# The sample's recurrence beside the prompt's projections, and half of w_out fetched during the prompt's recurrence

## The chip, the core and the metric

The kernel is one program on one core of a Trainium2 chip. The metric is the device time of one execution in microseconds; the time before is the median of three executions. The engines are TensorE (PE, the matrix products), VectorE (DVE), ScalarE (ACT), GpSimd (POOL) and SyncE (SP); SP and POOL issue nearly all of the transfers between the chip's main memory and the engines' memory.

## What is computed

A trunk of two layers runs over two requests with the same weights: a prompt of 1024 rows and a sample of 256 rows, 1024 columns each, all in float32. The sample doesn't depend on the prompt. In one layer:

```python
h = rms_norm(x, norm1_w[l])
proj = h @ w_in[l]                      # 1024 x (5*640 + 3*384)
q_h, zf, zb, i_h, g_h, q_a, k_a, v_a = split(proj)
hg_out = hgrn2_mixer(q_h, zf, zb, i_h, g_h, ...)    # gated recurrence, both directions, 5 heads of 128
at_out = dilated_attention_mixer(q_a, k_a, v_a)     # windowed attention, 3 groups of 2 heads
x = x + concatenate([hg_out, at_out]) @ w_out[l]
x = x + expert_choice_moe(rms_norm(x, norm2_w[l]), ...)   # 16 experts, each takes its best rows
```

The recurrence needs of `w_in` the columns q_h, zf, zb (640 each), of the same rows the values i_h and the gates g_h, and gives 640 of the 1024 columns that go into `w_out`; the attention gives the other 384.

## The kernel before

A product in float32 accuracy is made of three faster ones: each operand X is split into a rounded part H (made by ACT) and a rest L (made by DVE), and PE adds H·H, H·L and L·H. So a weight block costs a load (`raw`, `wr` or `or`), an ACT pass (`wH`, `oH`) and a DVE pass (`wL`, `oL`), and each product is three matmuls per 128 rows of depth.

`mixers` issues one layer's first half in this order. The program is written as streams (Python generators); `lanes` and `run_all` take from each stream in turn by an estimate of when its next PE work can start, and that fixes the order of each engine's instructions. Every engine and every queue of transfers then works through its own instructions strictly in that order. A stream that has to wait for another yields in `until` on a key of a dictionary.

1. **Projections** (`project`, L517, with `value_tile` L545 and `qkv_tile` L558). Four column blocks of 320 (values and gates of the recurrence, `mm<-wH,hTh` with 128x320 outputs) and three of 384 (attention) for both requests, a tile of 128 rows at a time: 8 tiles of the prompt, 2 of the sample. Results go to `vgp`, `vgs`, `qkvp`, `qkvs` in main memory. `order` lists the blocks; the sample runs some blocks ahead.
2. **The prompt's recurrence** (`hgrn` L578, `hgrn_task`, `hgrn_unit`), 5 heads times 2 units of 512 rows. A unit projects its own q and z (`mm<-hTh,wH`, 128x512, with the head's weights from `load_head` L593, whose raw tile `wr` has one buffer), then goes through levels: `lv<-qk`, five times `lv<-Q,km`, then `lv<-Q,K`, then a 128-row level, each of which waits for DVE products (`update`) and an ACT copy (`km`) of the one before; then states S, and outputs `tp<-v,A` and `tp<-S,Q`. They are squared, normalised (`hss`, `rs*`), multiplied by the gates `sg` (loaded at L648, one buffer) into `hob`, and stored by POOL (L1108) as `mbp`. Two units run at a time. Beside it run the 30 **attention** units (24 of the prompt, 6 of the sample), paced by `int(i * 0.2)` against the recurrence's progress `first`; their results are stored by SP (L930) as `obp`, `obs`.
3. **The sample's recurrence**, the same with 5 units of 256 rows (`lv<-hTh,wH`, 128x256). It waits for `projected` (the prompt's last projection is done) and `attended` (all attention is issued), so it starts about where the prompt's last unit has its levels, and goes on into the next stage. `out_weights` (L939) makes `oH` and `oL` from 16 loads of w_out through two `or` buffers at the same time.
4. **The output projection** (`out_proj` L979, `row_tile`): for each of 8 prompt tiles, then 2 sample tiles, load the mixed rows (`mix<-mbp` L1000, `obr<-obp` L1002, `x` L1005, by SP), weigh the attention (`aM`, `aw`), transpose, split (`mTh`, `mTl`), multiply by w_out (`mm<-oH,mTh`), add, norm, router logits. After the prompt's 8 tiles comes its expert choice (`topk_merged`, first instruction MAX8), then the experts.

Lines that most DVE and ACT instructions carry are those of a helper (L111); PE's are L182 (matmul) and L196 (transpose).

## Time and profile before

| | us |
|---|---|
| time, median of three executions (3395.47 to 3405.37) | 3402.97 |
| span of the profiled execution, first to last instruction | 3399.2 |
| PE busy in it | 3255.7 (96%) |
| DVE busy | 2113.0 (62%) |
| ACT busy | 1763.4 (52%) |
| mean granted TensorE clock, as a share of full speed | 0.978 |

The profile holds the span alone and no time around it; the span lies within the range of the timed executions, 3.8 us under their median. Matmuls overlap, so the duration shown for one is longer than its distance to the next: the cost of a row of equal matmuls is read from their starts. The stages in the span, by the first and last instructions of each kind: projections 26 to 290, the prompt's recurrence 290 to 634, the stretch up to the first product with w_out 634 to 704, the rest of the output projection up to the expert choice 704 to 869; in the second layer the last two are 2315 to 2388 and 2388 to 2556.

### The profile page before, as it was taken

The page shows a single profiled execution, that of the slowest core. Times are in us where ns is not written, and L with a number is a line of the kernel's source. Part 1 is how long each engine was busy: PE and PEld are TensorE (multiplying, and loading weights), DVE is VectorE, ACT ScalarE, POOL GpSimd, SP SyncE. Part 2 cuts the span into 40 slices and gives each one's busy share as a digit, 9 for nine tenths or more (in the row PEclk, how much of TensorE's full clock was granted, in tenths as well). Part 3 has the DMA queues.
Part 4 walks back from the last instruction along what each step waited for, and adds up shares of the span by engine and source line. Part 5 has one row for each costly group of instructions (what it writes and reads, how often), then busy time and mean ns, then how long its engine had stood idle before and what let it go on. Part 6 is the DMA issues. An engine that isn't in the chain of part 4 may idle for free.

```text
span 3399.2 us, 59013 instructions
## 1 busy us (share of the span) xinstructions
PE 3255.7 (96%) x23714; PEld 2485.4 (73%) x23714; DVE 2113.0 (62%) x4201; ACT 1763.4 (52%) x2533; POOL 270.4 (8%) x225
## 2 busy tenths in 40 slices
PE   8999999889899999999999999998997999999996
PEld 8998777777666667666699977777775666667664
DVE  5322677885866666666543137788757766666666
ACT  4214774553356666566532156745424665666665
POOL 0000000000111111111100000000001111111102
PEclk9999999899899999999999999998998999999998
DMA  5213222344498889888642132214434988888887
GB/s 180 91 56 89 64 75 60 113 149 127 171 326 281 286 284 323 297 281 284 218 149 89 55 101 67 65 48 134 146 122 170 325 319 287 284 286 312 303 284 251
DMA packets 423969, 641.88 MB, mean 189 GB/s; under 512 B 31376, under 2 KB 191760, under 8 KB 423696
## 3 DMA queue, kind: packets, MB, share of 16 engines
q1 hardware_dynamic: 398544, 557.88, 47.3%
q0 software_dynamic: 24432, 77.61, 8.3%
q8 instruction: 187, 3.06, 0.4%
q10 hardware_dynamic: 720, 2.62, 0.2%
q14 instruction: 86, 0.70, 0.1%
HBM read 551.13 MB, written 86.89 MB: 188 GB/s over the span
## 4 chain that ended last, share of the span: by engine, by line
PE 42%; DVE 3%; DMA 3%; ACT 1%; issue 1%; SPq 0%; POOLq 0%; ACTq 0%; DVEq 0%
PE mm L182 22%; PE lv L182 9%; PE sc L182 6%; PE tp L196 3%; PE tp L182 2%; DMA wr<-in_w_in_dram 1%; DVE wL L111 1%; DMA obr<-obp 0%; ACT wH L111 0%; DVE raw L111 0%; DVE ind L111 0%; DMA xbp<-ye,idxp 0%; DVE val L111 0%; DVE lv L111 0%; DMA xeS<-xns,gidx 0%
## 5 line engine op out<-in xcount | busy, mean ns | idle before, releaser
L111 DVE TENSOR_TENSOR wL<-raw,wH 128x2048 fp32r<-128x2048 f32 (+2 forms) x412 | 917.2, 2244 | 401.6 <-ACT wH L111 401.4
L111 ACT ACTIVATE wH<-raw 128x2048 fp32r<-128x2048 f32 (+2 forms) x412 | 774.4, 1882 | 189.1 <-PE mm L182 92.6
L182 PE MATMUL mm<-wH,hTh 128*128 128x320 f32 (+1 forms) x1120 | 361.1, 323 | 1.4 <-ACT hTh L111 1.3
L182 PE MATMUL mm<-wL,hTh 128*128 128x320 f32 (+1 forms) x1120 | 359.9, 321 | 0.3 <-DVE wL L111 0.3
L182 PE MATMUL mm<-wH,hTl 128*128 128x320 f32 (+1 forms) x1120 | 359.6, 321 | 0.0
L182 PE MATMUL sc<-raw,xs 128*32 128x512 f32 x2048 | 230.9, 597 | 0.0
L182 PEld LDWEIGHTS mm<-wH,hTh 128*128 128x128 f32 x1120 | 210.6, 188 | 2.3 <-ACT hTh L111 2.3
L182 PEld LDWEIGHTS mm<-wL,hTh 128*128 128x128 f32 x1120 | 210.6, 188 | 0.5 <-DVE wL L111 0.5
L182 PEld LDWEIGHTS mm<-wH,hTl 128*128 128x128 f32 x1120 | 210.5, 188 | 0.3 <-DVE hTl L111 0.2
L182 PE MATMUL mm<-wL,xh 128*128 128x512 f32 x512 | 205.3, 401 | 1.6 <-DVE wL L111 1.6
L182 PE MATMUL mm<-wH,xh 128*128 128x512 f32 x512 | 205.4, 401 | 0.0
L182 PE MATMUL mm<-hTh,wH 128*128 128x512 f32 x480 | 203.0, 423 | 0.0
L182 PE MATMUL lv<-wL,xh 128*128 128x512 f32 x512 | 200.1, 391 | 2.1 <-DVE wL L111 2.1
L182 PE MATMUL mm<-wH,xl 128*128 128x512 f32 x512 | 201.1, 393 | 0.0
L182 PE MATMUL lv<-wH,xh 128*128 128x512 f32 x512 | 199.5, 390 | 0.0
L182 PE MATMUL lv<-wH,xl 128*128 128x512 f32 x512 | 199.5, 390 | 0.0
L182 PE MATMUL mm<-hTh,wL 128*128 128x512 f32 x480 | 199.0, 415 | 0.3 <-DVE wL L111 0.3
L182 PE MATMUL mm<-hTl,wH 128*128 128x512 f32 x480 | 196.4, 409 | 0.0
L1264 POOL DMA_INDIRECT xbs<-yS,sidx x64 | 101.8, 1591 | 1120.5 <-ACT yS L111 976.5
L182 PEld LDWEIGHTS sc<-raw,xs 128*32 128x32 f32 x2048 | 64.4, 110 | 147.4 <-issue 144.7
L182 PE MATMUL sc<-raw,hs 128*32 128x512 f32 x1024 | 150.6, 598 | 0.0
L111 DVE TENSOR_TENSOR K<-K,TT 128x256 f32<-128x256 f32 (+1 forms) x360 | 126.1, 376 | 30.1 <-PE lv L182 19.1
(291 smaller groups left out, 6486.0 us busy)
## 6 DMA issues: line engine op xcount, KB each, us to landing
raw<-in_w_up_dram SPq DMA_DIRECT2D x128, 1024.0 KB, 15.6
raw<-in_w_down_dram SPq DMA_DIRECT2D x128, 1024.0 KB, 9.4
raw<-in_w_gate_dram SPq DMA_DIRECT2D x126, 1024.0 KB, 13.8
wr<-in_w_in_dram SPq DMA_DIRECT2D x60, 512.0 KB, 4.0
raw<-in_w_in_dram SPq DMA_DIRECT2D x16, 640.0 KB, 5.7
vgp<-vgo SPq DMA_DIRECT2D x64, 160.0 KB, 1.8
raw<-in_w_in_dram SPq DMA_DIRECT2D x12, 768.0 KB, 5.3
qkvp<-qo SPq DMA_DIRECT2D x48, 192.0 KB, 1.9
```

The source lines that it names most:

```text
L111: return fn(out, *args, **kw)
L182: self.last_mm = self.nc.tensor.matmul(out, lhsT, rhs, start=start, stop=stop)
L196: ins = self.nc.tensor.transpose(out, src, self.ident[:k, :k])
L1264: nc.gpsimd.indirect_dma_start(out=xs2, out_offset=at, in_=yS[64 * h:64 * h + 64], in_offset=None, compute_op=OP.add)
```

## The change

- `project` yields within its tiles (`mm3` becomes the stream `mm3y`), and the sample's recurrence runs beside it, right after the prompt's rows are normalised: a new state of two keys, `v` and `g`, tells it when the sample's values and gates are stored. The sample's fourth block is moved into the middle of the prompt's third.
- The sample's recurrence is gone from behind the prompt's. Its head weights use the projections' `raw` buffers (two, which were three); the prompt's still use one `wr`. The order of heads is now sample first, then prompt.
- Attention is paced by `min(10, int(i * 0.4))`, which leaves units 25 to 29 waiting for the prompt's last unit.
- `out_weights` has eight `or` buffers instead of two and issues the first eight loads at the start of the prompt's recurrence; all 16 passes of ACT and DVE still come after `projected`.
- The pools (regions of on-chip memory) are entered in another order.

The docstrings and comments that the change deletes are left out of this diff.

```diff
@@ mixers
-            hTs = self.new_hT(gs, left.enter_context(pool("hTs")))
-            proj = ExitStack()
+            proj, projs, blk = ExitStack(), ExitStack(), ExitStack()
             hTp = self.new_hT(gp, proj.enter_context(pool("hTp")))
-            with pool("rawA", "right") as rw, pool("wA", "right") as wa, \
-                    pool("stage", "right") as sp, pool("norm1", "right") as xp:
-                wp = (rw, 3, wa, 4)
+            hTs = self.new_hT(gs, projs.enter_context(pool("hTs")))
+            rw, wa, sp = (blk.enter_context(pool(n)) for n in ("rawA", "wA", "stage"))
+            state = dict(normed=0, all_normed=0, v=0, g=0, s=0, best=0, started=0, turned=0, multiplied=0, ended=0,
+                         projected=0, attended=0, scanned=0, loaded=0, p=0, merged=0)
+            wp = (rw, 2, wa, 4)
+            with pool("norm1", "right") as xp:
...
-                state = dict(normed=0)
-                self.run_all(self.project(l, hTs, hTp, sp, wp, first, state, 2),
-                             self.norm_in(l, gp, hTp, xp, w1, junk, state))
+                projecting = self.project(l, hTs, hTp, sp, wp, first, state, 2)
+                self.run_until(state, ("all_normed",), projecting, self.norm_in(l, gp, hTp, xp, w1, junk, state))
...
-            gp.next, gs.next = gs, None
+            self.head_raw = rw, "raw", 2
+            gs.next, gp.next = gp, None
+            gp.ps, gp.ps_name, gs.ps, gs.ps_name = self.mmp, "mm", self.lvp, "lv"
             for j in range(3):
-                self.load_head(l, gp, 0, j)
+                self.load_head(l, gs, 0, j)
+
+            def sample_hgrn():
+                with pool("hgrns", "right") as hg:
+                    yield from self.hgrn(l, gs, hTs, hg, ready=state)
+
+            self.run_all(sample_hgrn(), projecting)
+            blk.close()
+            projs.close()
...
+            orw = right.enter_context(pool("orw", "right"))
...
             def load_weights():
-                yield from self.until(state, "projected", 1)
-                yield from self.out_weights(l, *weights[0])
+                yield from self.out_weights(l, orw, weights, state)
                 state["loaded"] = 1
-            def sample_hgrn():
-                yield from self.until(state, "projected", 1)
-                yield from self.until(state, "attended", 1)
-                with pool("hgrns") as hg:
-                    yield from self.hgrn(l, gs, hTs, hg)
-                state["s_scanned"] = 1
...
@@ project
+        order.remove((3, gs))
+        order = [(b, g, range(g.T)) for b, g in order]
+        n = order.index((2, gp, range(gp.T)))
+        order[n:n + 1] = [(2, gp, range(0, 4)), (3, gs, range(gs.T)), (2, gp, range(4, 8))]
...
+            if g is gs and b in (1, 3):
+                state["v" if b == 1 else "g"] = 1
@@ value_tile, qkv_tile
-        self.mm3(ps, self.top(hT, P * i, P), self.wop(blk, 0, 320))
+        yield from self.mm3y(ps, self.top(hT, P * i, P), self.wop(blk, 0, 320))
@@ load_head
-        raw = wp.tile([P, 8, P], F32, name="wr")
+        rp, nm, bufs = self.head_raw
+        raw = rp.tile([P, 8, P], F32, name=nm, bufs=bufs)
@@ hgrn_task
         yield 150.0
+        yield from self.until(hd["ready"], "g", 1)
@@ hgrn_unit
         yield from self.until(state, "tails", (i - 2) // NU + 1)
+        yield from self.until(hd["ready"], "v", 1)
...
+        if NU == 1:
+            yield from self.until(state, "tails", i)
@@ attention
-            yield from self.until(scan, "first", int(i * 0.2))
+            yield from self.until(scan, "first", min(10, int(i * 0.4)))
@@ out_weights
-            raw = pool.tile([P, 512], F32, name="or", bufs=2)
+            raw = pool.tile([P, 512], F32, name="or", bufs=8)
...
-        load(0)
-        load(1)
-        yield 3000.0
+        for i in range(8):
+            load(i)
+        yield from self.until(state, "projected", 1)
+        H, L = weights[0]
         for i in range(16):
...
-            if i < 14:
-                load(i + 2)
+            if i < 8:
+                load(i + 8)
```

Where the order of instructions changes (first layer). **PE in the prompt's projections**, where values and gates are made; before, one tile after another:

```order
600 L182 MATMUL mm<-wH,hTh 128x320
601 L182 MATMUL mm<-wL,hTh 128x320
602 L182 MATMUL mm<-wH,hTl 128x320
603 L182 MATMUL mm<-wH,hTh 128x320
604 L182 MATMUL mm<-wL,hTh 128x320
```

PE at the same place now, where `lv`, `tp<-v,kt` and `tp<-ident,K` belong to the sample's recurrence:

```order
486 L182 MATMUL mm<-wL,hTh 128x320
487 L182 MATMUL mm<-wH,hTl 128x320
488 L182 MATMUL tp<-v,kt 128x128
489 L196 MATMUL tp<-ident,K 128x128
490 L182 MATMUL lv<-Q,km 32x32 x8
491 L182 MATMUL mm<-wH,hTh 128x320
492 L182 MATMUL mm<-wL,hTh 128x320
493 L182 MATMUL mm<-wH,hTl 128x320
```

The sample's level products stand 6 to 26 projection matmuls apart, and its last unit ends 732 matmuls ahead of the end of the projections.

**PE from the first level of the prompt's last unit on**; before, the sample's projections (128x256) stand between the levels:

```order
2855 L182 MATMUL lv<-hTl,wH 128x256
2856 L182 MATMUL lv<-hTh,wL 128x256
2857 L182 MATMUL lv<-qk 32x32 x16
2858 L182 MATMUL lv<-hTh,wH 128x256
2859 L182 MATMUL lv<-hTl,wH 128x256
2860 L182 MATMUL lv<-hTh,wL 128x256
```

Now what stands between the last levels is the last attention units (`qkvr`, `kT`, `sc`, `qT`):

```order
3252 L182 MATMUL lv<-Q,K 32x32 x9
3253 L196 MATMUL tp<-ident,qT 128x128
3254 L182 MATMUL lv<-Q,K 32x32 x7
3255 L196 MATMUL tp<-ident,qkvr 128x128 x2
3256 L182 MATMUL sc<-kT,qT 128x128 x2
3257 L182 MATMUL lv<-Q,km 128x128 x4
3258 L196 MATMUL tp<-ident,qkvr 128x128 x2
3259 L196 MATMUL tp<-ident,K 128x128 x2
3260 L182 MATMUL sc<-kT,qT 128x128 x2
3261 L196 MATMUL tp<-ident,K 128x128
```

And on PE the output projection's first transposes (`mix`) follow the unit's last outputs at once:

```order
3281 L182 MATMUL tp<-S,Q 128x128 x2
3282 L182 MATMUL tp<-v,A 128x128
3283 L182 MATMUL tp<-S,Q 128x128
3284 L196 MATMUL tp<-ident,mix 128x128 x4
3285 L182 MATMUL mm<-oH,mTh 128x512
```

Between the last unit's `lv<-qk` and these transposes there are 50 attention matmuls, and none of the sample's recurrence.

**SP's queue at the end of the prompt's recurrence**; before, w_out's and the sample's weight loads come ahead of the first mixed rows:

```order
184 L604 DMA wr<-in_w_in_dram 128x8x128 x2
185 L950 DMA or<-in_w_out_dram 128x512 x2
186 L604 DMA wr<-in_w_in_dram 128x8x128
187 L950 DMA or<-in_w_out_dram 128x512 x3
188 L648 DMA sg<-vgp 128x4x128
189 L950 DMA or<-in_w_out_dram 128x512
190 L761 DMA v<-vgs 128x2x128
191 L604 DMA wr<-in_w_in_dram 128x8x128
192 L1000 DMA mix<-mbp_85 128x512
```

SP at the same place now:

```order
181 L967 DMA or<-in_w_out_dram 128x512 x8
182 L863 DMA qkvr<-qkvs 16x3x128 x5
183 L947 DMA obs<-ao 128x132
184 L947 DMA obs<-ao 64x132 x4
185 L863 DMA qkvr<-qkvs 16x3x128 x3
186 L947 DMA obs<-ao 16x132 x16
187 L662 DMA sg<-vgp 128x4x128
188 L1018 DMA mix<-mbp_85 128x512
189 L1018 DMA mix<-mbp_86 128x128
190 L1020 DMA obr<-obp 128x3x132
```

The second half of w_out's loads stands ahead of the last attention unit's loads, and the attention's last 16 stores stand ahead of the last gates and the first mixed rows. The number of PE instructions is the same before and after (18266).

## Rows read from the trace of the kernel before

**Rows 1.** The page: the span.

```profile
span 3399.2 us, 59013 instructions
```

**Rows 2.** Busy time by stretch: start:end, length, engines busy (x instructions), PEclk, DMA share, GB/s.

```profile
100.00:150.00 50.00, 50.00 (x343) 50.00 (x342) 17.68 (x32) 8.99 (x16) 0.00 (x0) 1.00 0.28 94
295.90:302.70 6.80, 6.80 (x26) 5.63 (x26) 3.27 (x12) 5.40 (x16) 0.00 (x0) 0.50 0.57 161
...
634.00:704.30 70.30, 50.67 (x720) 45.02 (x720) 58.28 (x188) 34.20 (x72) 4.20 (x6) 0.84 0.52 155
2315.40:2387.80 72.40, 52.32 (x717) 46.13 (x717) 62.98 (x195) 36.00 (x74) 3.51 (x5) 0.79 0.48 140
704.30:869.20 164.90, 160.68 (x1253) 125.48 (x1254) 107.35 (x440) 67.80 (x166) 11.53 (x20) 0.99 0.40 127
2387.80:2556.40 168.60, 162.24 (x1253) 125.23 (x1254) 108.44 (x456) 66.96 (x164) 12.25 (x21) 0.98 0.41 128
```

**Rows 3.** The chain of waits, second layer, 2310 to 2400: start us, us, what.

```profile
2325.17 4.62 DMA wr<-in_w_in_dram
```

**Rows 4.** PE's timeline in the output projection: start us, us, instruction, x pieces.

```profile
720.36 0.39 PE L182 MATMUL tp<-v,A 128*128 128x128 f32 x2
...
721.35 0.33 PE L182 MATMUL lv<-Q,km 128*32 128x32 f32 x16
...
722.19 0.28 PE L182 MATMUL lv<-hTl,wH 128*128 128x256 f32 x1
...
724.43 0.28 PE L182 MATMUL lv<-hTh,wL 128*128 128x256 f32 x1
...
728.99 0.28 PE L182 MATMUL lv<-hTh,wH 128*128 128x256 f32 x1
729.20 0.33 PE L182 MATMUL lv<-Q,km 128*32 128x32 f32 x16
...
729.69 0.28 PE L182 MATMUL lv<-hTh,wL 128*128 128x256 f32 x1
```

**Rows 5.** The sample's matmuls ahead of 634 (580 on) and of 2315.4 (2260 on).

```profile
L182 PE MATMUL lv<-hTh,wH 128*128 128x256 f32 x13 | 3.7, 287 | 0.0
...
L182 PE MATMUL lv<-hTh,wH 128*128 128x256 f32 x15 | 4.1, 276 | 0.0
```

**Rows 6.** PE's timeline: router's last matmul of two tiles, two tiles apart.

```profile
837.83 0.38 PE L182 MATMUL sc<-ident,re 128*16 128x128 f32 x2
...
868.46 0.39 PE L182 MATMUL sc<-ident,re 128*16 128x128 f32 x2
```

**Rows 7.** DVE by form, 634 to 690: xcount | busy us, mean ns | idle before.

```profile
L111 DVE TENSOR_TENSOR oL<-or,oH 128x512 fp32r<-128x512 f32 x14 | 9.4, 684 | 0.0
...
L111 DVE TENSOR_TENSOR K<-K,TT 128x256 f32<-128x256 f32 x12 | 4.6, 418 | 0.1
L111 DVE TENSOR_TENSOR Q<-Q,TT 128x512 f32<-128x512 f32 x6 | 4.1, 681 | 0.0
...
L111 DVE SCALAR_TENSOR_TENSOR S<-S,T 128x128 f32<-128x128 f32 x9 | 2.7, 345 | 0.0
```

**Rows 8.** Timelines of ACT, DVE and POOL behind the prompt's last outputs [idle before <-releaser].

```profile
680.10 1.09 ACT L111 ACTIVATE hob<-tp 128x512 f32<-128x512 f32 x2 [0.36 <-PE tp L182]
...
690.35 1.13 DVE L111 SCALAR_TENSOR_TENSOR hob<-tp,rsy,sg 128x128 f32<-128x128 f32 x4 [0.33 <-DMA sg<-vgp]
...
692.01 0.75 POOL L1108 DMA_DIRECT2D mbp<-hob  x1 [3.51 <-ACT S L111]
...
2380.34 0.75 POOL L1108 DMA_DIRECT2D mbp<-hob  x1 [3.51 <-DVE K L111]
...
2389.64 0.16 DVE L111 TENSOR_TENSOR aM<-obr 128x2 f32<-128x2 f32 x1 [1.08 <-DMA obr<-obp]
```

**Rows 9.** DMA issues, 634 to 704: xcount, KB each, median us to landing.

```profile
obr<-obp SPq DMA_DIRECT2D x2, 198.0 KB, 8.2
sg<-vgp SPq DMA_DIRECT2D x1, 256.0 KB, 3.0
```

More of the change, by code (lines that the diff above doesn't have):

```diff
@@ L87 @@
 class Wait(float):
+    pass
 class Engine:
@@ L445, in after_projections @@
                 op = left.enter_context(pool("wout"))
-                weights.append((op,) + tuple(op.tile([P, 8, D], F32R, name=n) for n in ("oH", "oL")))
+                weights.append(tuple(op.tile([P, 8, D], F32R, name=n) for n in ("oH", "oL")))
                 state["projected"] = 1
@@ L484, in mixers @@
                 pools = tu, no, mi, wo
-                gens = [hgrns, self.out_proj(l, gp, pools, weights[0][1:], consts, state),
-                        sample_rest(pools, consts), self.topk_merged(l, gp, no, state), loading]
-                self.run_all(*[gens[i] for i in (4, 0, 1, 3, 2)])
+                self.run_all(loading, self.out_proj(l, gp, pools, weights[0], consts, state),
+                             self.topk_merged(l, gp, no, state), sample_rest(pools, consts))
     def new_hT(self, g, pool):
@@ L528, in get @@
                 parts[b] = self.wblk(blocks[b][2], wp)
-        for n, (b, g) in enumerate(order):
+        order.remove((3, gs))
+        order = [(b, g, range(g.T)) for b, g in order]
+        n = order.index((2, gp, range(gp.T)))
+        order[n:n + 1] = [(2, gp, range(0, 4)), (3, gs, range(gs.T)), (2, gp, range(4, 8))]
+        for b, g, tiles in order:
             get(b)
-            for i in range(g.T):
+            for i in tiles:
                 if g is gp:
@@ L539, in project @@
                 if kind == "v":
-                    self.value_tile(g, hT, parts[b], part, i, pool, nw)
+                    yield from self.value_tile(g, hT, parts[b], part, i, pool, nw)
                 else:
-                    self.qkv_tile(g, hT, parts[b], part, i, pool)
+                    yield from self.qkv_tile(g, hT, parts[b], part, i, pool)
                 yield 0.0
+            if g is gs and b in (1, 3):
+                state["v" if b == 1 else "g"] = 1
     def value_tile(self, g, hT, blk, b, i, pool, nw):
@@ L560, in qkv_tile @@
         ps = self.mmp.tile([P, AW], F32, name="mm")
-        self.mm3(ps, self.top(hT, P * i, P), self.wop(blk, 0, AW))
+        yield from self.mm3y(ps, self.top(hT, P * i, P), self.wop(blk, 0, AW))
         o = pool.tile([P, 6, 64], F32, name="qo", bufs=2)
@@ L576, in qkv_tile, with hgrn @@
                           o.rearrange("p a b -> p (a b)"))
-    def hgrn(self, l, g, hT, pool, after=None, state=None):
+    def hgrn(self, l, g, hT, pool, after=None, state=None, ready=None):
         NU = g.nt // g.unit
@@ L581, in hgrn @@
         state = state or dict(levels=0, first=0, tails=0)
+        ready = ready or dict(v=1, g=1)
         for h in range(HH):
-            hd = dict(h=h, units={}, state=state, after=after if h == HH - 1 else None)
+            hd = dict(h=h, units={}, state=state, ready=ready, after=after if h == HH - 1 else None)
             for u in range(NU):
@@ L939, in attention, with out_weights @@
         yield from self.lanes(tasks, width)
-    def out_weights(self, l, pool, H, L):
+    def out_weights(self, l, pool, weights, state):
         nc = self.nc
```

12 lines of the change are left out of this document (5 added, 7 removed).

## The prediction

> **What bounds the kernel now.** I read the busy times by stretch first [rows 2]. In the projections PE is busy in all 50 of 50 us and DVE in 17.7 of them. Between the first level of the prompt's last unit (634.0 and 2315.4) and the first product with w_out (704.3 and 2387.8) PE works 50.7 of 70.3 us and 52.3 of 72.4 us, at a mean clock of 0.84 and 0.79. In the output projection behind that it is full again, but the sample's recurrence is still in it. So the change moves work from a stage with holes into one that has none, and what it can win is 20 us of idle time in each layer and what the clock loses there. The chain of waits names the cause of the holes: a head's raw weights, `wr`, have one buffer, and each load (4.62 us) begins when the DVE pass on the one before is done [rows 3]. The changed kernel has no such load in that stretch. Then I look at single instructions, to price the sample's PE work and the chain that remains. The experts' stage, most of the span, is untouched.
>
> The sum is made against the profiled span, 3399.2 us [rows 1], which is 3.8 us under the median of the runs; I add the difference to the median.
>
> **What is added: the sample's recurrence in the projections.** PE's price at full clock, per layer:
> - 5 heads by 3 blocks by 24 matmuls make 360 of 128x256. From 722.19 to 724.43 there are 19 steps, 0.118 us each [rows 4]: 42.4 us.
> - 7 groups of 32x32 in each of 5 units. A group and the two matmuls behind and before it take from 728.99 to 729.69; less two steps of 0.118, that is 0.46 us with the switching [rows 4]. 35 of them: 16.3 us.
> - 10 pieces of 128x128 in each unit, at (721.35 − 720.36) / 4 = 0.25 us [rows 4]: 12.4 us.
>
> Together 71 us, in a stage where PE is the bound, so all of it is paid. What I cost at nothing there: the DVE and ACT passes (PE hides them, DVE has 32 of 50 us free), the 15 head loads, and the waits from one level to the next. 343 matmuls in 50 us are 0.146 us each [rows 2]; 6 to 26 of them between two of the sample's levels cover 0.9 to 3.8 us. If that cover is too short, it is the third rival.
>
> **What is removed.** From 704.3 to 869.2 the output projection takes 164.9 us and from 2387.8 to 2556.4 168.6 us [rows 2]. Two tiles late in the stage, with nothing of the sample beside them, take 868.46 − 837.83 = 30.6 us [rows 6], so 8 tiles take 122.5 us; 3.5 us more for the first tile's transposes and the last one's router make 126. The rest, 38.9 and 42.6 us, goes. The sample's matmuls that stood ahead of the last unit go too: 39 and some 44 (three forms, one row each) at 0.118 us [rows 5], 4.6 and 5.2 us. The 70.3 and 72.4 us between are replaced by a new tail, E.
>
> **What is moved.** Five attention units, 50 matmuls, leave the full part of the recurrence for the tail: at about 0.2 us (many have 64 rows or columns) 10 us less ahead of it. At the end of the projections PE was fully busy for 6.8 us at half clock in the stretch at 295.9 [rows 2], which cost 3.4 us; the same comes in the second layer. Now the first head's weights are ready sooner, but the attention's first transposes wait as before. Between 0 and 3.4 I take 1.7 us in each layer. w_out's eight early loads I cost at nothing: in the old tail DVE waited for `oH` or `or` in none of the 14 passes (idle 0.0) [rows 7], so they took no time that could be won. What they cost if that is wrong is SP's time of issue, hidden behind 340 us of recurrence.
>
> **The new tail E**, from the last unit's `lv<-qk` to the running output projection. It has two parts.
> - DVE's part. In its order stand 16 passes `oL` at 0.684, 14 products K at 0.418, 7 products Q at 0.681 with 0.5 more for the strided one, 9 of S at 0.345 [rows 7]: 10.9 + 5.9 + 5.3 + 3.1 us. Masks and T make about 5, the five attention units about 5 by an estimate from their instructions. Sum 35. Below it stands what the same chain needs with half of the passes out of its way, some 29; above it 46, which is 634.0 to the squares at 680.10 in the old tail [rows 2, 8], where the sample's levels took DVE as well. I take 35, because the sample's levels are gone.
> - The closing chain. In the old tail the squares begin at 680.10 and the second half's store at 692.01 [rows 8]: 11.9 us, with the sample's work in between. Its floor is squares 1.1, norm about 3.3, `hob` 1.1, then the second `sg`, whose only buffer becomes free with the first `hob`, 3.0 [rows 9], and `hob` 1.1 again: 9.6 us. I take the floor. From that store to the first product there were 12.3 us in the first layer (to 704.3), and 9.3 us to `aM` in the second (2389.64, which waits for `obr`) [rows 2, 8]; `obr` took 8.2 us to land [rows 9]. I keep both. About 3 us of transposes and products are done within the last wait.
>
> E is 35 + 9.6 + 12.3 − 3 = 53.9 us, and 50.9 us in the second layer. PE has only some 22 us of work in it: the tail has more holes than before, and it is shorter all the same. What is late next is DVE, then the chain of store, `mix` and `obr`.
>
> **Sum.** First layer: 53.9 − 70.3 − 38.9 − 4.6 − 10 − 1.7 + 71 = −0.6. Second layer: 50.9 − 72.4 − 42.6 − 5.2 − 10 − 1.7 + 71 = −10.0. Together −10.6 us: span 3388.6, and 3392 against the median. The unknown is E: at a mean of 57.7 us instead of 52.4 nothing is left.
>
> **Rivals.**
> - *Short tail.* Durations on DVE overlap, part of `oL` falls into waits between levels, and in a tail with few transfers `obr` lands sooner. For it: SP issues a third less there. E is then 9 to 10 us less, at 44 and 41: −30 us, 3373. Against it: the passes are in one queue with the levels.
> - *Half clock in the tail* (the slower side). In the old tail PE was busy for 72% of the time and its clock was still 0.84 and 0.79 [rows 2], so half speed (1.2 instead of 2.4 GHz) had a third of it and more; in the new one it is busy for 22 of 53 us. Its place is the tail's PE pieces: 7 level groups, transposes, states, outputs, attention. At half speed their 22 us become 44; I put half of the 22 more on the chain, since the rest falls into waits for DVE: E +11 in each layer, +11 us in all, 3414. It decides from +5.3 us a layer on, a good quarter of the pieces' extra time. Against it: DVE, not PE, sets the pace of the levels, and the old tail paid it as well. The Trainium skill, page TensorE: Matmul & The Clock Gate, section HAM oscillation, has this as a rule: a wait for data between bursts of matmuls drops the clock to half, and each burst then begins cold. It speaks against the change; the two clocks of the old tail agree with it, while the stretch at 295.9 shows half clock with PE fully busy.
> - *Levels that wait in the projections.* PE takes its instructions in order, so a level product that is not ready holds the projections back. There are 9 steps in a unit, 90 in both layers; 0.45 us of wait at each is +40 us: 3433. It decides from 0.12 us a step. For it: the shortest cover is 0.9 us, less than one step's products and copy. Against: most covers are 12 matmuls and more, 1.8 us, and DVE and ACT have little else to do there.
> - *Nothing gained*: the stage ends as before because other waits fill the place: 3403.
>
> **How the numbers follow.** Forecast 0.55 (E within 6 us either way, 3380 to 3404), short tail 0.17, half clock 0.18, waits in the projections 0.07, nothing 0.03. A measurement of this kernel tells about 0.3% from no change, 10 us. Half of the forecast case is beyond that, with the short tail 0.46 faster. The other half of it, the nothing and a little of the half clock are 0.32 within. The rest, 0.22, is slower. The range, 3366 to 3416, takes in the short tail and the half clock and leaves out the waits in the projections and the ends of both.
>
> **What would show it.** The projections of each layer 71 us longer, with PE as full as before and hardly any wait of PE for `km` or K. From the last unit's `lv<-qk` to the first `mm<-oH,mTh` 50 to 57 us, with DVE busy in nearly all of the first 35 and two holes of PE, for `sg` and for `obr`. The output projection 126 us. The prediction is wrong if PE's clock in the tail is under 0.7 with PE's pieces on its chain, if the projections grow by over 80 us, or if DVE waits in the tail for the last attention unit's loads, which stand behind eight loads of w_out in SP's queue.

## The result, and the profile after

| | before | changed |
|---|---|---|
| time, median (runs) | 3401.01 us (3395.47 to 3405.37) | 3434.41 us (3431.44 to 3437.38) |
| ratio, 95% interval | | 1.0094 [1.0078, 1.0111] |
| span of the profiled execution | 3399.2 us | 3433.2 us |
| mean granted TensorE clock | 0.978 | 0.972 |

The changed kernel is 0.9% slower. 3392 was predicted, range 3366 to 3416; the time lies above the range.

The stages, by the starts of the same instructions in both traces (in the second layer counted from its own start, which comes 17.4 us later than before):

| us | before | changed | difference | predicted |
|---|---|---|---|---|
| projections | 291.6 / 279.6 | 362.6 / 352.1 | +71.0 / +72.5 | +71 / +71 |
| recurrence, to the last unit's `lv<-qk` | 342.4 / 340.0 | 323.1 / 322.9 | −19.3 / −17.1 | −16.3 / −16.9 |
| tail E, to the first product with w_out | 70.3 / 72.4 | 52.5 / 53.5 | −17.8 / −18.9 | −16.4 / −21.5 |
| output projection, to MAX8 | 164.9 / 168.6 | 139.6 / 140.2 | −25.3 / −28.4 | −38.9 / −42.6 |
| MAX8 to the first expert's products done | 51.2 / 51.2 | 60.4 / 61.3 | +9.2 / +10.1 | 0 / 0 |

The first four lines come to +8.6 and +8.1 us: taking the sample out of the second half of the stage saves 62.4 and 64.4 us and putting it into the first costs 71.0 and 72.5. The last line is a second loss, in a stage of which the change moves nothing.

Busy times by stretch in the changed kernel (start:end, length, PE, PEld, DVE, ACT, POOL, granted clock, DMA share, GB/s): inside the projections, the tail of either layer, and the output projection of either layer. They answer to [rows 2].

```profile
100.00:150.00 50.00, 50.00 (x383) 49.30 (x382) 15.48 (x39) 9.57 (x19) 0.00 (x0) 1.00 0.23 77
...
685.70:738.20 52.50, 34.67 (x382) 25.58 (x381) 36.51 (x127) 26.97 (x72) 1.56 (x3) 0.67 0.23 67
2388.20:2441.70 53.50, 34.21 (x382) 24.67 (x381) 37.43 (x129) 26.90 (x72) 1.64 (x3) 0.67 0.22 66
738.20:877.80 139.60, 129.02 (x701) 96.43 (x702) 68.65 (x258) 36.55 (x95) 10.51 (x19) 0.94 0.43 141
2441.70:2581.90 140.20, 129.15 (x701) 96.46 (x702) 68.64 (x258) 36.53 (x95) 10.43 (x19) 0.94 0.44 140
```

The projections are as full as before, so every matmul put there is paid in full. The tail's clock is 0.67, where the old one had 0.84 and 0.79. In the output projection PE is idle for 10.6 and 11.1 us; with the sample beside it, it was for 4.2 and 6.4.

Where these 10 us lie, the first 27 us behind the first product show:

```profile
738.20:750.20 12.00, 5.21 (x13) 3.39 (x14) 3.07 (x14) 0.33 (x2) 1.93 (x3) 0.50 0.72 227
750.20:765.20 15.00, 14.87 (x69) 11.88 (x71) 10.06 (x50) 4.30 (x14) 0.56 (x1) 0.86 0.50 147
```

For 12 us PE works 5.2, at half clock; then it is full. VectorE's timeline there (start, us, instruction; in brackets the idle time before it and what ended it), which answers to the last row of [rows 8]:

```profile
740.39 0.16 DVE L111 TENSOR_TENSOR aM<-obr 128x2 f32<-128x2 f32 x1 [2.97 <-DMA obr<-obp]
...
740.87 0.69 DVE L111 TENSOR_TENSOR mTl<-tp,mTh 128x512 fp32r<-128x512 f32 x1
747.33 0.29 DVE L111 TENSOR_TENSOR wr<-wr,wc 128x128 f32<-128x128 f32 x1 [5.78 <-DMA wr<-in_w_router_dram]
...
748.53 0.56 DVE L111 TENSOR_TENSOR mix<-obr,aw 128x384 f32<-128x384 f32 x1
```

and TensorE's in the same place:

```profile
736.39 1.09 PE L196 MATMUL tp<-ident,mix 128*128 128x128 f32 x4 [8.65 <-DMA mix<-mbp]
738.22 0.79 PE L182 MATMUL mm<-oH,mTh 128*128 128x512 f32 x1 [0.74 <-ACT mTh L111]
...
741.61 0.79 PE L182 MATMUL mm<-oH,mTl 128*128 128x512 f32 x1 [2.17 <-DVE mTl L111]
...
749.14 1.12 PE L196 MATMUL tp<-ident,mix 128*128 128x128 f32 x4 [4.60 <-DVE mix L111]
```

VectorE stands for 5.8 us before the router's weights (`wr`), which the first tile needs only 17.5 us later; behind that instruction in its queue stand the steps that make the attention's part of `mix`, and for those TensorE waits 4.6 us. POOL issues the load of `wr` after the tail's last store `mbp`:

```profile
737.39 0.75 POOL L1126 DMA_DIRECT2D mbp<-hob  x1 [3.56 <-issue]
738.13 0.55 POOL L322 DMA_DIRECT2D w<-in_norm_w_dram  x1
738.68 0.56 POOL L987 DMA_DIRECT2D rev<-in_c_rev_dram  x1
739.23 0.90 POOL L990 DMA_DIRECT2D wr<-in_w_router_dram  x1
```

The old kernel had the same order, but there the first product (704.3) came 12.3 us behind that store and 10.5 us behind the load, VectorE's instruction on `wr` (703.71 and 2390.32) found it there without a wait, and the sample's work kept PE full in the first 15.7 us:

```profile
693.84 0.90 POOL L972 DMA_DIRECT2D wr<-in_w_router_dram  x1
```

```profile
704.30:720.00 15.70, 15.68 (x111) 12.21 (x112) 13.55 (x57) 7.92 (x21) 0.00 (x0) 0.86 0.71 217
```

The second new loss lies at the experts. SP's first loads of their weights, before and after:

```profile
867.87 1.15 SPq L266 DMA_DIRECT2D raw<-in_w_gate_dram  x2
```

```profile
917.61 0.94 SPq L266 DMA_DIRECT2D raw<-in_w_gate_dram  x2
```

and the waits of SP's queue in 860 to 940 of the changed kernel (waiting line, waited for: total, times, longest), with ScalarE's first pass on those weights:

```profile
SPq L266 <- DMA xns<-xn: 52.0, 2, 42.4
```

```profile
925.24 1.91 ACT L111 ACTIVATE wH<-raw 128x2048 fp32r<-128x2048 f32 x1 [9.69 <-DMA raw<-in_w_gate_dram]
```

Before, the loads were issued 1.3 us ahead of MAX8 (869.2), now 39.8 us behind it (877.8): they wait for the store of the normed rows of the sample's last tile. Nothing in the code orders the two. That they share memory three of the first four experiments show: eight buffers `or` in place of two push the pools behind them, and the first raw tile comes to lie on those rows.

### The profile page after: what moved, and what is told of

It reads as the page before. It is cut to its first block, busy times and chain, and to the rows that moved or that the text cites. A ratio compares the mean times of both kernels' runs of the same rounds, so it can differ in the third digit from the quotient of the medians.

```text
span 3433.2 us, 59012 instructions
## 1 busy us (share of the span) xinstructions
PE 3264.8 (95%) x23714; PEld 2482.6 (72%) x23714; DVE 2129.7 (62%) x4201; ACT 1726.7 (50%) x2507; POOL 270.6 (8%) x225
## 4 chain that ended last, share of the span: by engine, by line
PE 43%; DVE 3%; DMA 2%; ACT 1%; issue 1%; SPq 0%; POOL 0%; POOLq 0%; ACTq 0%; DVEq 0%
PE mm L182 22%; PE lv L182 10%; PE sc L182 6%; PE tp L196 3%; PE tp L182 2%; DMA raw<-in_w_up_dram 1%; DMA raw<-in_w_in_dram 0%; ACT wH L111 0%; DVE ind L111 0%; DVE wL L111 0%; DVE val L111 0%; DVE raw L111 0%; DMA wr<-in_w_router_dram 0%; DMA obr<-obp 0%; ACT xn L111 0%
## 5 line engine op out<-in xcount | busy, mean ns | idle before, releaser
L111 DVE TENSOR_TENSOR wL<-raw,wH 128x2048 fp32r<-128x2048 f32 (+2 forms) x448 | 961.2, 2162 | 400.4 <-ACT wH L111 398.7
L111 ACT ACTIVATE wH<-raw 128x2048 fp32r<-128x2048 f32 (+2 forms) x448 | 812.6, 1816 | 258.4 <-PE lv L182 112.6
```

The costliest lines, as they stand in the source:

```text
L111: return fn(out, *args, **kw)
```

## Experiments

Each run is compared with before on the same chip. "Experts" is MAX8 to the first expert's products done, "run-in" the first product with w_out to the first router matmul, "squares" the last `lv<-qk` to ScalarE's first squares, each for both layers. The changed kernel has experts 60.4 / 61.3, run-in 26.9 / 26.6, squares 41.6 / 42.7. A run-in can be set beside another only where as many products stand in it: 56 in the changed kernel and the other runs, but 65 in **pace** and **warm**, whose edits also changed PE's order there. For these two the stretch from the squares to MAX8 says more; it is 150.5 / 151.0 in the changed kernel.

### Why the experts' weights come late

**rotate**: other raw buffers first.

```diff
+            for _ in range(4):
+                rawp.tile([P, 4, 512], F32, name="raw", bufs=8)
             wp = (rawp, 8, wp, 4)
```

> The changed kernel, with one edit: the ring of eight buffers for the experts' raw weights starts four buffers further on, so that the first expert's loads go to memory that the prompt's head weights and w_out's raw tiles held, and not to that of the sample's last normalised rows. Theory (place): in the changed kernel the expert stage starts 9.3 and 10.1 us later behind the expert choice only because these loads wait for that memory (they were issued at 917.6, after the store of the sample's last rows; before the change at 867.9). Then the edit gives back 17 to 20 us: 3434 becomes 3414 to 3417, and the first loads are issued by 880. Rival (busy): the expert stage starts later since the expert choice and the sample's last tiles are themselves later against the prompt's; then the edit changes nothing, 3434.

Measured 3433.11 us, ratio 1.0083 [1.006, 1.0105], experts 60.0 / 59.0. The loads still came behind the same wait. The expectation of 880 for them failed (916.4). Whether the edit moved the first loads to other memory at all the run doesn't show, so it decides nothing.

**or2**: two `or` buffers, as before.

```diff
-            raw = pool.tile([P, 512], F32, name="or", bufs=8)
+            raw = pool.tile([P, 512], F32, name="or", bufs=2)
...
```

> The changed kernel without its prefetch of w_out: two raw buffers for w_out as before the change, two loads at the start of the prompt's recurrence, the rest behind the passes. Theory (place): the prefetch's 12 KB more per partition pushed the pools behind it over the memory of the first expert loads; with two buffers the layout there is that of before, and the expert stage starts 9 to 10 us earlier in each layer, 3434 becomes 3414 to 3417; the tail itself doesn't grow, since no pass on w_out waited for its load before. Rival (loads): the prefetch is worth something, each of 14 loads that now stand behind a pass holds DVE's queue for up to 1 us, and the tail grows by 5 to 14 us in each layer: 3425 to 3445.

Measured 3417.12 us, 1.0043 [1.003, 1.0057], experts 51.1 / 50.8, the level of before. The tail grew to 56.2 / 57.3 and the run-in fell to 22.5 / 25.1; the two together are 0.7 us shorter and 2.3 us longer than in the changed kernel. So little are the six more early loads of w_out worth here.

**or2pad**: the same with 12 KB per partition of memory that nobody uses, so that the pools lie where eight buffers put them.

```diff
+            nc.vector.memset(orw.tile([P, 3072], F32, name="pad")[:, 0:1], 0.0)
```

> The kernel of the run or2 (two raw buffers for w_out) with an unused tile of 12 KB beside them, so that every pool behind lies where it lies in the changed kernel, while w_out's loads are still late. Theory (place): the first expert loads wait again for the memory of the sample's last normalised rows, the expert stage begins 59 to 61 us behind the expert choice instead of 51, and the time goes from 3417 back to 3434 to 3438. Rival (traffic): it was the eight early loads themselves that made the expert stage late; without them it stays at 51 and 3417.

Measured 3437.4 us, 1.0098 [1.0081, 1.0114], experts 60.3 / 60.0. With two buffers and without the six early loads, place alone brings the whole loss back, and with it the wait of SP's queue (860 to 940):

```profile
SPq L266 <- DMA xns<-xn: 51.9, 2, 42.4
```

**place**: eight buffers, the pools opened in another order.

```diff
-            with pool("turned", "right") as tu, pool("normed", "right") as no, pool("mixed", "right") as mi, \
-                    pool("tail", "right") as wo:
+            with pool("normed", "right") as no, pool("mixed", "right") as mi, pool("turned", "right") as tu, pool("tail", "right") as wo:
```

> The changed kernel with one edit: the four pools that hold the attention's normed, mixed and turned rows and the tail's weights are opened in the order normed, mixed, turned, tail, so that the first expert's raw weights come to lie on memory that is given back before the sample's last tile is done. All eight buffers of w_out stay. Theory of the memory's place: the gate and up weights of the first expert are issued some 10 us or more before the 917.6 of the changed kernel (868 before), the step from the router's last choice to the first expert's products falls from 60.3 and 60.0 back to about 51, the tail's 52.5 and 53.5 and the 139.6 and 140.2 of out_proj stay, and the time falls by 18 to 20, to 3412 to 3418. Rival, that eight early loads of w_out themselves crowd the queue: the step stays near 60 and the time near 3434.

Measured 3420.19 us, 1.0038 [1.0027, 1.005]. The loads go out at 900.5 for 917.6:

```profile
900.53 0.94 SPq L266 DMA_DIRECT2D raw<-in_w_gate_dram  x2
```

The experts take 53.2 / 53.3 for 60.4 / 61.3, short of the expected 51, and no other stage moves by more than some 2 us. Against the ratio of the changed kernel that is −0.0056, 19 us, as expected. The last three runs settle the place. Counted from MAX8 (877.2 here) the loads come 23.3 us behind it for 39.8; these 16.5 us win back 7 to 8 of the 9 to 10 us, and the 24.6 us by which they are still later than before go with the other 2.

### What the run-in waits for

**router**: the router's weights in memory of their own, loaded ahead of the recurrence (six `or` buffers to make room).

```diff
+            early = self.router_consts(l, right.enter_context(pool("early", "right")))
...
-                consts = self.tail_consts(l, wo)
+                consts = self.row_bcast(wo, self.I["norm2_w"][l], D, "w2", queue=nc.gpsimd), early
```

> The changed kernel, with the router's weights, the reversal matrix and the rows for the affinities in a pool of their own ahead of the prompt's recurrence, loaded and multiplied there; w_out's raw buffers are six instead of eight to make room. Theory (queue): in the first tile of the output projection DVE stood 5.8 us before the product with the router's weights, whose load could only be issued when the recurrence's pool was free, and the weights of the attention rows and the second half of the split are queued behind it; without it the stretch from the first product with w_out to the first MAX8 goes from 139.6 and 140.2 to 133 to 135 us, and the time from 3434 to 3421 to 3425. Rival (clock): these 14 us are the half clock and the lack of other work for PE, and the wait hides in it: at most 2 us a layer, 3430 to 3434.

Measured 3428.15 us, 1.0071 [1.0047, 1.0095], run-in 21.8 / 22.6. VectorE's 5.8 us for `wr` are gone, and 4.4 of them come back at `obr`; since other waits lay beside these, the output projection gets 4.4 and 2.7 us shorter. The time lies between what the two theories expected. VectorE's waits at 725 to 766 in this run:

```profile
DVE aM L111 <- DMA obr<-obp: 8.0, 3, 3.7
```

where the changed kernel has

```profile
DVE wr L111 <- DMA wr<-in_w_router_dram: 5.8, 1, 5.8
DVE aM L111 <- DMA obr<-obp: 3.6, 2, 3.0
```

**obr**: `obr` loaded ahead of `mix`.

```diff
+            ob = mixed.tile([P, 3, 132], F32, name="obr", bufs=2)
+            nc.sync.dma_start(ob, g.ob[:, rows, :].rearrange("g t c -> t g c"))
             mx = mixed.tile([P, D], F32, name="mix", bufs=2)
...
```

> The changed kernel, with the attention's rows of a tile (obr) loaded ahead of the recurrence's (mix) instead of behind them. Theory (queue): DVE's 2.97 us wait for obr goes, but the product with the router's weights still stands behind it in the queue until their load lands, so almost nothing is won: 3431 to 3435. Rival (obr): the load of obr, which stands behind that of mix on SP and so behind the store of the recurrence's last half, is what holds the first tile: 3 to 6 us less in each layer, 3422 to 3428.

Measured 3435.69 us, 1.0098 [1.0074, 1.0122]. `aM` came 2.4 and 3.0 us earlier, counted from the last `lv<-qk`, and the time didn't fall: VectorE still had `wr` ahead. Two waits in one queue, each of which hides the other.

**all2**: both, with two `sg` buffers and two `or` buffers (shown is the edit of `sg`; the others are as above).

```diff
-            sg = pool.tile([P, C, P], F32, name="sg", bufs=1)
+            sg = pool.tile([P, C, P], F32, name="sg", bufs=2 if g.name == "p" else 1)
```

> The changed kernel with four edits: two raw buffers for w_out (layout of before), the router's weights ahead of the recurrence, obr loaded ahead of mix, and two buffers for the prompt's gates sg. Theory (queue and place): the waits are one behind the other in the first tile and in the closing chain; taken away together they give 6 to 10 us in each layer beyond the run or2: 3397 to 3405, level with the kernel before. Rival (clock): the stores, mix and a cold PE take their place, and at most 3 us in each layer are left of it: 3411 to 3417.

Measured 3416.07 us, 1.004 [1.0028, 1.0053], in the range of the rival and not of the theory. The run-in fell to 16.0 / 17.4 and the output projection to 129.3 / 131.3; PE is busy for 15.88 of the first 16 us. But the tail grew to 58.1 / 60.2: the waits now lie ahead of the first product, where PE stands still for 15.4 us. With two buffers w_out's last loads stood in SP's queue behind the attention's 16 stores, and `obr` behind them:

```profile
718.79 7.34 SPq L948 DMA_DIRECT2D obs<-ao  x16
726.23 7.26 SPq L968 DMA_DIRECT2D or<-in_w_out_dram  x3
```

From the squares to MAX8 all2 takes 146.6 / 149.3 for 150.5 / 151.0. So of the 10.3 and 8.9 us by which the output projection is shorter only 3.9 and 1.7 are won, and the experts take 3.4 and 3.7 back (54.5 / 54.5 for 51.1 / 50.8 in **or2**).

### What sets the first part of the tail

**nol**: the eight subtractions `oL` of w_out's second half left out.

```diff
+        nc.gpsimd.memset(L[:, 4:8].bitcast(F32), 0.0)
...
-            nc.vector.tensor_tensor(L[at], raws[i], H[at].bitcast(F32), OP.subtract)
+            if i < 8:
+                nc.vector.tensor_tensor(L[at], raws[i], H[at].bitcast(F32), OP.subtract)
```

> The changed kernel without the lower part of the second half of w_out: the eight subtractions oL on VectorE that make it are left out and its place is filled with zeros once, so that part of the product is missing; all matmuls stand as they were. It asks what bounds the first part of the tail, from the last prompt qk to the squares (41.6 and 42.7 in the changed kernel, 35 predicted). Theory that VectorE's work bounds it: eight passes at 0.6 to 0.7 us go, the squares come at 36 to 38, the tail falls by about 5 per layer, and the time to about 3424. Theory that TensorE at half clock bounds it: the squares stay at 41 to 43, the tail within 1 of 52.5 and 53.5, and the time within 3 of 3434.

Measured 3437.66 us, 1.0093 [1.0069, 1.0118], squares 41.9 / 43.7. VectorE does 4.2 us less in this stretch and the end doesn't move.

**noh**: `oH` and `oL` of that half left out, both set to zero.

```diff
...
+            if i < 8:
+                nc.scalar.activation(H[at], raws[i], AF.Copy)
+                self.after_all()
+                nc.vector.tensor_tensor(L[at], raws[i], H[at].bitcast(F32), OP.subtract)
```

> The changed kernel without the second half of w_out: eight roundings oH and eight subtractions oL are left out, and both halves of that part are zeros, so that its part of the product is missing; all matmuls and all loads stand. Theory of ScalarE's queue: the squares come at 36 to 38, the time is 3422 to 3427. Theory of TensorE at half clock: they stay at 40.5 or more, the time within 4 of 3434. A value between (38 to 40.5) says that both have a share.

Measured 3439.94 us, 1.0105 [1.0088, 1.0122], squares 41.1 / 43.8. ScalarE too works 4 us less, to no effect.

**late8**: no work left out, the last eight passes of both engines moved behind the last unit's levels.

```diff
         for i in range(16):
+            if i >= 8:
+                yield from self.until(scan, "tails", 5)
...
```

> The changed kernel with the last eight passes oH on ScalarE and oL on VectorE held back until the last unit's levels are through; the same work, eight passes of each moved behind the last mask. Theory that ScalarE's queue bounds the first part of the tail: up to 8 times 0.63, or 5 us, leave the road between the levels, the squares come at 36.5 to 39 in place of 41.6 and 42.7, and the time falls to 3424 to 3430. Theory that TensorE at half clock bounds it (33 us of its 41.6): the squares stay within 1.5 of 41.6 and 42.7, and the time within 4 of 3434. Should the passes then stand in the way of the states behind the levels, the squares come later, at 44 to 46, and the time is 3438 to 3442.

Measured 3434.21 us, 1.0088 [1.0071, 1.0105], squares 43.2 / 41.8. The three runs say the same: w_out's passes don't hold the chain up.

**pace**: attention paced as before, so that its last five units are done ahead of the tail.

```diff
-            yield from self.until(scan, "first", min(10, int(i * 0.4)))
+            yield from self.until(scan, "first", int(i * 0.2))
```

> The changed kernel with the attention paced as before the change (0.2 a unit), so that the last five units no longer wait for the prompt's last unit. The prediction: the recurrence ahead of the last unit grows by 10 us in each layer, and the tail loses only the attention's 5 us on DVE; 3434 becomes 3442 to 3446. Rival (order): in the tail the attention's stores and loads on SP and its work on DVE hold the chain, and without them the tail is 10 us or more shorter: 3425 to 3434.

Measured 3444.2 us, 1.0118 [1.0101, 1.0135]. Squares 33.2 / 30.9, and the recurrence 333.4 / 333.5 for 323.1 / 322.9: the squares come 8.4 and 11.8 us nearer to the last `lv<-qk`, and 10.3 and 10.6 us come back ahead of it. Nor does all of the 8.4 and 11.8 reach the next stage: the first product comes 59.3 and 56.9 us behind the last `lv<-qk`, for 52.5 and 53.5, because in this run's order a second row of transposes stands ahead of it on PE. It waits for VectorE, which stands 3.0 us before `obr` and 5.7 before `wr` meanwhile:

```profile
750.88 1.09 PE L196 MATMUL tp<-ident,mix 128*128 128x128 f32 x4 [11.75 <-DVE aM L111]
```

From the squares to MAX8 the run takes 155.0 and 155.8 us; 4.0 and 7.0 us are left of the gain at MAX8. The busy time of the engines between the last `lv<-qk` and the squares, in the changed kernel, in **nol** and in **pace**:

```profile
685.70:727.30 41.60, 33.15 (x376) 24.61 (x376) 30.29 (x91) 25.29 (x69) 0.00 (x0) 0.67 0.23 64
```

```profile
684.80:726.70 41.90, 34.26 (x376) 25.45 (x376) 26.06 (x83) 25.16 (x69) 0.00 (x0) 0.63 0.22 64
```

```profile
695.80:729.00 33.20, 19.53 (x281) 17.17 (x267) 25.30 (x60) 14.22 (x28) 0.00 (x0) 0.54 0.22 65
```

13.6 us of PE's time less bring the end 8.4 us nearer; 4.2 us of VectorE's bring nothing. But **pace** takes with the attention 11.1 us of ScalarE's work and 5.0 of VectorE's out of this stretch too, and a wait of PE for the attention's rows (2.8 us in the changed kernel). So it shows that the attention's pieces lie on the chain, and not that TensorE alone does.

**warm**: 48 products without use on TensorE between the last unit and the output projection, to hold its clock.

```diff
+            t = self.scp.tile([P, 512], F32, name="sc")
+            for _ in range(48):
+                self.mm(t, weights[0][0][:, 0, 0:P], weights[0][0][:, 0, 0:512])
```

> The changed kernel with 48 added products on w_out's finished first block, without use, on PE: 16 of them scatter through the end of the recurrence, 32 stand in the hole ahead of the first mixed rows, 7 us at full clock. Theory (queue): the first tile of the output projection waits for DVE's queue (obr, router's weights) and not for PE, so a PE at full clock wins at most 1.5 us a layer: 3431 to 3436. Rival (clock): the 14 us that the first tile takes too long are half clock; with the clock at 1.0 when its first product comes, the stretch to the first MAX8 goes from 140 to 132 to 135, and the time to 3420 to 3427.

Measured 3448.61 us, 1.0138 [1.0121, 1.0155], outside both ranges. The run-in is 19.1 / 19.0 and the tail 67.3 / 68.3. The products themselves cost little: 32 of them ran at full clock in the hole and were done before the first mixed rows came. What came late is the first product. In this run's order a second row of transposes stands ahead of it, and it waits 11.96 us for VectorE, which waits 5.3 of them for `wr`:

```profile
726.98 7.52 PE L182 MATMUL sc<-oH 128*128 128x512 f32 x32
735.77 0.63 PE L196 MATMUL tp<-ident,mix 128*128 128x128 f32 x4 [1.28 <-DMA mix<-mbp]
748.36 1.08 PE L196 MATMUL tp<-ident,mix 128*128 128x128 f32 x4 [11.96 <-DVE aM L111]
752.21 0.79 PE L182 MATMUL mm<-oH,mTh 128*128 128x512 f32 x1 [0.69 <-ACT mTh L111]
```

Behind that wait the clock was 0.50 again (752.2 to 757.0), so the run didn't bring about what it was to test. It doesn't tell what full clock alone would bring, and no run here does.

### The mended waits together

**best**: the pools' order of `place`, the router's weights early as in `router`, six `or` buffers. **best2**: also two `sg` buffers, with five `or` buffers. **bestlate**: `best` with the passes held back as in `late8`. To the edits shown above comes a little unused memory, so that the pools behind lie as in `place`:

```diff
+            with pool("pad", "right") as pd, pool("normed", "right") as no, pool("mixed", "right") as mi, pool("turned", "right") as tu, pool("tail", "right") as wo:
+                nc.vector.memset(pd.tile([P, 240], F32, name="pad")[:, 0:1], 0.0)
```

> The pools' order of the run 'place' together with the router's weights in memory of their own, loaded ahead of the recurrence as in the run 'router', and six buffers of w_out for eight. If the two costs are separate they add: the step to the first expert's products about 51, from the first out_proj matmul to the first router matmul 21 to 23 for 26.9, a tail of 52 to 55, so 18 to 20 and 6 less than 3434: 3407 to 3411. If the raw weights hang on the eight buffers rather than on the order, the step stays at 55 or more and the time over 3414.

> As the run 'best', with two sg buffers for the prompt's gate in place of one and five buffers of w_out. By the theory that sg's one buffer holds the first tile's hob back (3.2 us in the changed kernel), 2 to 3 us a layer less than 'best': 3402 to 3407, level with before (3402). Rival, that fewer buffers of w_out bring its last loads behind the sixteen stores of obs, as in the run with all small edits and two buffers: the tail grows to 56 to 60 per layer and the time is 3411 to 3418.

> The run 'best' with the last eight passes held back as in 'late8'. By the theory of ScalarE's queue 5 to 10 us less than 'best' (1.0035 of before): 0.9995 to 1.002 of before, which is level with it. By the theory of TensorE's half clock no gain: 1.003 to 1.0045. In neither case clearly faster than before, since the 142 us that the sample costs in the projections are already matched by what the rest gives back.

Measured: best 3418.55 us, 1.0035 [1.0024, 1.0046], run-in 22.2 / 23.9, experts 54.1 / 54.1; best2 3418.41 us, 1.0032 [1.002, 1.0044], tail 48.9 / 50.4, run-in 25.3 / 26.6; bestlate 3416.82 us, 1.0033 [1.0021, 1.0045]. By stage the two gains of best nearly add, though the experts stay 3 us above the expected 51, and its profiled span is 21.6 us under that of the changed kernel. But the profile is of the fastest of its ten executions, 5.2 us under their median. By its ratio its time is 3414 for a before of 3402, 3 to 7 us above the expectation, and only 1 us under place, which the intervals don't tell apart. In best2 the second `sg` brings the first product 3 us forward and the run-in takes the 3 us back: VectorE waits 7.8 us at a stretch for `obr` there, which is loaded behind `mix`. No version is faster than before: with both losses mended as far as they were, the sample costs 143.5 us in the projections of the two layers and still brings a little less behind them.

## Why the prediction was wrong

**Right: the price in the projections.** 71 us reckoned, 71.0 and 72.5 measured, from starts in the old output projection [rows 4]. (One term is a little too high: the 0.99 us there hold eight pieces of 128x128, 0.12 us each, and the trace of the changed kernel has 90 of them in the projections of a layer, 11.1 us for 12.4.) TensorE's waits in 26 to 362 of the changed kernel (the longest and the only one for `km`):

```profile
PE lv L182 <- DVE TT L111: 1.6, 1, 1.6
...
PE lv L182 <- ACT km L111: 0.5, 1, 0.5
```

So the rival of levels that wait in the projections fell. That its 3433 is the measured time is chance.

**Right: what is moved, and the cost of w_out's early loads.** The recurrence got shorter by 19.3 and 17.1 for 16.3 and 16.9. In the first layer part of the difference is the clock, which stays full (1.00 from 362.6 to 369.4) where [rows 2] shows half of it behind the projections; 1.7 of those 3.4 us had been reckoned. The early loads cost nothing as transfers, since or2pad without six of them takes as long (1.0098 for 1.0094); what they cost was memory.

**Wrong: "8 tiles take 122.5 us; 3.5 us more" make 126.** Measured 139.6 and 140.2, 13.6 and 14.2 too many. From the first router matmul on the stage takes 112.7 and 113.6, which leaves 13.3 of the 126 for the run-in, and that took 26.9 and 26.6. The period of two late tiles [rows 6] says nothing on the first, whose waits no other tile's products cover. The step that failed is "The rest, 38.9 and 42.6 us, goes": 25.3 and 28.4 went. In the old stage the sample's work kept PE full while the first rows came; without it PE stands still for 10.6 and 11.1 us of the stage.

Not all of the 13.6 and 14.2 us is new, though. The sum kept the old 12.3 and 9.3 us from the second store to the first product, and they became 0.8 and 0.9: the first products need only the first four heads' half of `mix`. The waits for the other half, which the sum had ahead of the first product, lie behind it, in the run-in. From the squares to MAX8, where the boundary doesn't matter, the sum has 144.9 and 141.9 us, and 150.5 and 151.0 were measured: 5.6 and 9.1 too many. With the wait for `wr` gone (**router**) it is 146.0 and 148.3.

**Wrong: "The experts' stage, most of the span, is untouched."** It starts 9.2 and 10.1 us later. No line of it was changed, and no instruction in it was moved. The pools' new layout made its first loads wait, and the pools' new order, which the list of the change names, was given no price in the prediction. This is the largest single error. place takes 15 of these 19 us away by order alone.

**Right in sum by luck, wrong in its parts: the tail.** 53.9 and 50.9 predicted, 52.5 and 53.5 measured: the first part came out 6.6 and 7.7 us longer than its 35, and the wait behind the second store 11.5 and 8.4 us shorter. "DVE's part" of 35 us was 41.6 and 42.7, and VectorE was not its bound. The chain of waits in the second layer's stretch, 2388.2 to 2430.9, is TensorE for 25.1 us, ScalarE for 8.5 and VectorE for 7.0; `oL`, a third of the predicted 35, has 0.7 us of it. Its longest pieces (start, us, what):

```profile
2395.52 1.61 PE sc L182 x6
2398.32 2.12 ACT sc L111 x10
2402.53 1.48 PE tp L182 x12
2410.52 2.02 PE lv L182 x8
2426.74 4.08 PE tp L182 x34
```

All of these but the last are the attention's pieces or the levels they share PE with. The prediction had PE at "some 22 us of work": 33.15 us at a clock of 0.67 are 22.2 at full clock, so the amount was right and the speed was not. An estimate from the chain: a third of its 25.1 us, 8 us, is due to the clock, and 42.7 less 8 is the predicted 35 by another road. So the half clock rival named the likely mechanism, and its price of 11 us in each layer was some 8; the sign that the prediction set for it, a clock under 0.7 with PE's pieces on the chain, came. That the clock and not the attention's order makes the 6.6 and 7.7 us is argued from the chain; no run raised the clock there. The Trainium skill, page TensorE: Matmul & The Clock Gate, section HAM oscillation, has half clock come from a wait for data between bursts of matmuls. The trace agrees behind the closing chain: TensorE stood 8.65 us for `mix`, and its clock was 0.50 in the 12 us from the first product on. In the first part of the tail it doesn't show that picture: TensorE was busy for 33.15 of 41.6 us there, and its longest wait was 2.8 us.

The closing chain took 10.1 and 10.0 us where 9.6 was the floor taken, and the 3 us that the sum took off for work done within the last wait didn't come.

**The account.** 44.6 us lie between the predicted span, 3388.6, and 3433.2. The experts' first loads are 19.3 of them, the stretch from the squares to MAX8 14.7, the first part of the tail 14.3, the projections 1.5, the recurrence −3.2, what is left −2.0.

**What stays open.** How much of the tail's first part full clock alone would save, and what the waits for `obr` that remain in best (8.2 us of VectorE's time from 720 to 766) still cost.

## What to carry to other kernels

Work that lies beside a stage with waits costs there only what the waits don't cover: before it is moved to a full stage, price the stage that it leaves as it will be without it, first tile included, and not by its steady period. A load that is issued far ahead is paid in memory: after any change in sizes or order of pools look at which first loads of the next stage now lie on the last rows of this one. And an in-order queue that waits for something needed only later (the router's weights ahead of the mixing) hides behind neighbours until these are gone. Where a program orders its instructions by estimates, an edit in one place can reorder others: before a stretch of two runs is compared, count what stands in it.

## What the runs showed of the hardware

Half clock came with TensorE far from idle: 33.15 of 41.6 us busy at a mean of 0.67, and in the five microseconds from 695.9

```profile
695.90:700.90 5.00, 4.19 (x52) 2.79 (x50) 5.00 (x14) 4.61 (x17) 0.00 (x0) 0.50 0.37 113
```

4.19 of 5.00 us at 1.2 GHz. [rows 2] had it at 0.50 with PE busy for 6.80 of 6.80 us. And a small load can take long: the router's weights, 64 KB, stand in the second layer's chain of waits for 7.88 us, where 640 KB of `w_in` take a median of 4.4 by the page:

```profile
2442.65 7.88 DMA wr<-in_w_router_dram
```

```profile
raw<-in_w_in_dram SPq DMA_DIRECT2D x16, 640.0 KB, 4.4
```

326 GB/s were moving in these 7.88 us, and POOL had issued a store of 256 KB and loads of 512 and 64 KB in the 2 us ahead. Which of the two makes the load late no run tells.
